# Sums of the activations on VectorE from reloaded x, weight-sum transfers at 0.7 of their pace and a reordered product in a hybrid DeltaNet, GLA and forgetting-attention layer

## The chip, the cores and the metric

The kernel runs on one core of a Trainium2 chip (trn2). The metric is the device time of one execution in microseconds (us); smaller is better. The names of the engines in the profile are PE (TensorE, matmuls), PEld (its weight loads), DVE (VectorE), ACT (ScalarE), POOL (GpSimd) and SP (SyncE, which here only issues transfers). The core has 16 DMA engines. A queue name with a q (ACTq, POOLq, SPq) is an engine's instruction queue issuing a transfer.

## The reference

One layer normalises 16 meta tokens and 512 tokens of width 2048, projects them with one wide matrix, sends the columns to three mixers in parallel, gates and joins their outputs, projects again, adds the input and normalises.

```python
h = concatenate([meta, x])                      # 528 x 2048
h0 = rms_norm(h, norm_w)
proj = h0 @ w_in                                # all heads' q, k, v, z, gates
o_dn  = gated_delta_rule_chunked(...)           # 6 heads x 128, short conv + silu on q, k, v
o_gla = gla_chunked(...)                        # 5 heads, dk 64, dv 128
o_fox = forgetting_attention(q, k, v, log_f)    # 5 heads x 128, softmax with forget bias
o = concatenate([o_dn, o_gla, o_fox])           # each times silu of its own z
out = rms_norm(h + o @ w_out, final_norm_w)[16:]
```

Everything is float32.

## The kernel before, in words

**Operands.** x is kept transposed, as 16 tiles of 128 features x 528 tokens, each times norm_w and split exactly into two float32r parts `xh[k]` and `xl[k]`. A weight block is loaded in two halves of 128 x 1024 (`load_half`), each split into `whi` (ScalarE, line 162) and `wlo` (VectorE, line 163). A product is then three matmuls: hi by hi, hi by lo, lo by hi. Plain projections run through `inproj` (matmuls of line 220).

**Pairs of blocks.** From the second forgetting-attention head on, two blocks of w_in are multiplied at once by a Strassen-like scheme with seven products in place of eight (`inproj_pair`, matmuls of line 533, 24 a product and half the tokens, HT = 264). Four of the seven use sums of weight quarters, three of them sums of quarters of x. In x the quarters are feature tiles k and k + 8, first and second half of the tokens.

- The *sums of weights* are made by transfers alone, in memory: `steps_of` issues, from GpSimd's queue, plain copies (line 448) and accumulating transfers (line 446) into `ti` for w_in, and into `tw` for the output weights, which are used in the same way at the end of the kernel. Each of these transfers is 512 KB. They are spread by a price: every `load_half` adds `rate` to an account, a copy costs 1 and an accumulating transfer 1.6, and transfers are placed while the account is positive. `AHEAD` starts them with a rate of 2 at the first DeltaNet group.
- The *sums of x* (`x_sums(ks)`, tiles `t_k`, three sums t1, t2 and t4 for each of eight k) are made by GpSimd out of xh and xl with eight additions each (tile `xd`, line 490), then split by ScalarE (line 485) and VectorE (line 486). `XSUM` says where: two k's in each of the second and third GLA pair, four in the first forgetting head.
- A fourth sum replaces the second token half of `xh[k]`, `xl[k]` for k < 8 once the plain projections no longer need it (`x_last`): `x_last(False)` forms it on VectorE in head 0 (lines 513 to 515, tiles `xe`, `xf`), `x_last(True)` splits it into place in head 1 (lines 517, 518). The product that reads it, with `ti[n, 2]`, is the fifth of the seven; the one with `ti[n, 3]` is the sixth.

**Order.** The program is written engine by engine through one scheduler that orders the instructions of every engine when the kernel is built; at run time each engine takes its own in that order. Transfers issued by GpSimd, ScalarE and SyncE stand in these engines' queues among their other instructions. Buffers come from pools: tag "row" has 7 tiles of 128 x 531, tag "six" 14 larger ones; a tile that is asked for waits until one is free.

**Stages.** First the DeltaNet gates and keys, values and queries of the first three heads, the inverse of their triangular matrices (`dn_inverse`), and the mix; then the same for the last three. The inverse runs on VectorE on small tiles and passes twice through memory: `scr`, then `sc` to `iv` (lines 694, 697), after which line 702 transposes and TensorE's `pm` (line 708) follows. Then come GLA in three pairs (`gla_pair`: scores `pss`, states `pgn`, outputs `pgo`, `pgt`), beside projections that fill TensorE, then the five forgetting heads (`fox_head`). In a forgetting head each of four query blocks passes from `pfa`, `pfd` (scores, lines 1137, 1138) through VectorE (1141, 1143), ScalarE (1146) and VectorE (1147 to 1151) to `pfx` (transposes, 1154); then `pfo` (1170 to 1173) takes all blocks. The last stage is the output projection (line 1285).

Of the kernel before, what the change touches and what calls it, by code (L numbers as in the profile page):

```python
# [8 lines left out]
F32 = mybir.dt.float32  # L9
# [4 lines left out]
AF = mybir.ActivationFunctionType  # L14
ALU = mybir.AluOpType
# [3 lines left out]
P = 128  # L19
# [4 lines left out]
T = NM + S  # L24
HT = T // 2
# [10 lines left out]
H1 = 1  # L36
# [46 lines left out]
def tile_hybrid_trunk(ctx, tc, xT, xtok, mtok, w_gate, w_in, w_out, w_dn, consts, lmask, fin_w, out, dbg=None):  # L83
    nc = tc.nc
# [12 lines left out]
    def row(name, dt=F32):  # L97
        return wk.tile([P, 3 + T], dt, tag="row", bufs=7, name=name)
# [113 lines left out]
    xh, xl = [], []  # L212
# [259 lines left out]
    def x_sums(ks):  # L472

        three = {}
        for k in ks:
            three[k] = six.tile([P, 3, T], F32R, tag="six", name=f"t_{k}")
            V.memset(three[k][:, 0, 0:1].bitcast(F32), 0.0)
        for k in ks:
            o3 = three[k]
            t = row(f"xd{k}")  # L480
            a, b = t[:, :HT], t[:, HT:T]
            B = lambda part_, i, j: (xh, xl)[part_][k + 8 * i][:, HT * j : HT * j + HT].bitcast(F32)

            def parts(n, r, hi, lo, k=k):
                A.activation(hi, r, AF.Copy, scale=-1.0)
                V.scalar_tensor_tensor(out=lo, in0=r, scalar=-1.0, in1=hi.bitcast(F32), op0=ALU.mult,
                                       op1=ALU.subtract)
                xt_[n, k] = hi, lo

            two = lambda o, p_, q_, op=ALU.subtract: G.tensor_tensor(out=o, in0=p_, in1=q_, op=op)  # L490
            two(a, B(0, 0, 1), B(0, 0, 0))
            two(b, B(1, 0, 1), B(1, 0, 0))
            two(a, a, b, ALU.add)
            parts("t1", a, o3[:, 0, :HT], o3[:, 0, HT:])
            two(b, B(0, 1, 1), a)
            two(b, b, B(1, 1, 1), ALU.add)
            parts("t2", b, o3[:, 1, :HT], o3[:, 1, HT:])
            two(a, B(0, 1, 0), b)
            two(a, a, B(1, 1, 0), ALU.add)
            parts("t4", a, o3[:, 2, :HT], o3[:, 2, HT:])  # L500

    xr = {}

    def x_last(last):

        f = lambda u: u[:, HT:].bitcast(F32)
        if not last:
            t6 = six.tile([P, 6, HT], F32, tag="six", name="xe")
            t2 = row("xf")
        for k in range(NK):  # L510
            if not last:
                xr[k] = a = t6[:, k] if k < 6 else t2[:, HT * (k - 6) : HT * (k - 5)]
                V.tensor_tensor(out=a, in0=f(xh[k + 8]), in1=f(xh[k]), op=ALU.subtract)
                V.tensor_tensor(out=a, in0=a, in1=f(xl[k + 8]), op=ALU.add)
                V.tensor_tensor(out=a, in0=a, in1=f(xl[k]), op=ALU.subtract)
            else:
                A.copy(xh[k][:, HT:], xr[k])
                V.tensor_tensor(out=xl[k][:, HT:], in0=xr[k], in1=f(xh[k]), op=ALU.subtract)  # L518

    def inproj_pair(n, c1, c2, tmp):  # L520

        h, one, two = PAIRS[n]
        b1, b2 = BLOCK_OF[one, h], BLOCK_OF[two, h]
        ta, tb = tmp[:, :HT], tmp[:, HT:]
        bank = lambda i: psb.tile([P, 512], F32, tag="b", name=f"pp{b1}_{i}")
        lo_, hi_, dead = slice(0, HT), slice(HT, T), slice(NM, HT)

        def product(p_, src, xx, first=False, cols=slice(0, HT)):

            hi, lo = load_half(src, f"{b1}_{len(order)}")  # L530
            todo = [(hi, j, i) for j in range(NK) for i in range(2)] + [(lo, j, 0) for j in range(NK)]
            for i, (wt, j, part_) in enumerate(todo):
                m = PE.matmul(p_[:, cols], wt[:, j * P : (j + 1) * P], xx[j][part_][:, cols],  # L533
                              start=first and i == 0, stop=i == len(todo) - 1, skip_group_check=True)
                order.append(m.ins)

        xs_ = lambda ks, sl: [(xh[k][:, sl], xl[k][:, sl]) for k in ks]
        sums = lambda nm: [xt_[nm, k] for k in range(NK)]
        up, dn = range(NK), range(8, 8 + NK)
        a, b = bank("a"), bank("b")  # L540
        product(a, w_in[b1, 0], xs_(up, lo_), True)
        A.copy(ta, a[:, :HT])
        product(b, w_in[b1, 1], xs_(dn, lo_), True)
        V.tensor_tensor(out=c1[:, lo_], in0=b[:, :HT], in1=ta, op=ALU.add)  # L544
        product(a, ti[n, 1], sums("t2"))
        A.copy(tb, a[:, :HT])
        d = bank("d")
        product(d, ti[n, 0], sums("t1"), True)
        V.tensor_tensor(out=tb, in0=d[:, :HT], in1=tb, op=ALU.add)
        product(a, ti[n, 2], xs_(up, hi_))  # L550
        A.copy(ta, a[:, :HT])  # L551
        c = bank("c")
        product(c, ti[n, 3], xs_(dn, hi_), True)
        V.scalar_tensor_tensor(out=c2[:, hi_], in0=d[:, :HT], scalar=-1.0, in1=ta, op0=ALU.mult, op1=ALU.subtract)
        V.tensor_tensor(out=c1[:, hi_], in0=c[:, :HT], in1=tb, op=ALU.add)
        product(a, w_in[b2, 1], sums("t4"), cols=dead)
        A.activation(c2[:, dead], a[:, dead], AF.Copy, scale=-1.0)

# [496 lines left out]
    def fox_head(h):  # L1055
# [24 lines left out]
        if h < H1:  # L1080
            evac(inproj(("fk", h)), kT)
            v = row(f"vf{h}")[:, :T]
            evac(inproj(("fv", h)), v)
            x_sums(XSUM.get(3, ()))
            vhi, vlo, v3, vm = values(v)
            evac(inproj(("fq", h), meta=False), qT, scale=float(P) ** -0.5)
        else:
            n = 2 * (h - H1) - SKIP
            if n < 0:
                evac(inproj(("fk", h)), kT)  # L1090
                evac(inproj(("fq", h), meta=False), qT, scale=float(P) ** -0.5)
            else:
                inproj_pair(n, kT, qT, qk[:, 1])
                G.tensor_tensor(out=kT, in0=kT, in1=rstd, op=ALU.mult)
                V.scalar_tensor_tensor(out=qT[:, NM:], in0=qT[:, NM:], scalar=float(P) ** -0.5, in1=rstd[:, NM:],
                                       op0=ALU.mult, op1=ALU.mult)
            v = row(f"vf{h}")[:, :T]
            zr = row(f"zfz{h}")[:, :T]
            if h == H1:
                x_last(True)  # L1100
            inproj_pair(n + 1, v, zr, qk[:, 1])
            if h == FOX_HEADS - 1:
                for i in range(6):
# [18 lines left out]
        G.affine_select(out=cm, in_=cb[:, NM:].rearrange("p (b t) -> p b t", b=NB), pattern=[[0, NB], [-1, P]],  # L1122
                        base=0, channel_multiplier=1, compare_op=ALU.is_ge, fill=BIG)

        if h == H1 - 1:
            x_last(False)
        mt = t15(f"fmt{h}", (P, NB, 2, NM), F32R)
        pm = row(f"ptm{h}", dt=F32R)[:, :S]
        G.tensor_copy(pm, zero_c.to_broadcast([P, S]))
# [46 lines left out]
            nc.sync.dma_start(out=zd[DN_HEADS + GLA_HEADS + h], in_=z)  # L1176


    AHEAD = {(0, -1): (2, (-1, -2, -3, -4, -5, -6, -7), (0, 1, 2, 3))}
    XSUM = {1: (0, 1), 2: (2, 3), 3: (4, 5, 6, 7)}  # L1180
    PM = (308, 319)

    def ahead(g, i):
# [324 lines left out]
```

## Time and profile before

| | before |
|---|---|
| three runs | 1068.16, 1080.19, 1082.35 us |
| median | 1080.19 us |
| the profiled execution, its own time | 1075.85 us |
| its span, first to last instruction | 1074.1 us |
| mean granted TensorE clock in it | 0.971 |
| GpSimd's queue of transfers (q0), bytes | 46.14 MB |

Shares of busy time are averages over stages with different limits; what a stage is limited by is read from the waits in it. The rows of the profile give a group of instructions by line, engine and operation, with the tiles written and read; the timelines give start and duration in us, and in brackets the time that the engine had been idle before and what ended that. A window's row gives the busy time of each engine in a stretch of time.

### The profile page before, as it was taken

How to read it: one execution, taken by the hardware profiler on the slowest of the kernel's cores; microseconds unless marked ns; L12 is line 12 of the kernel's file. 1: busy time of each engine (PE TensorE's matmuls, PEld its weight loads, DVE VectorE, ACT ScalarE, POOL GpSimd, SP SyncE). 2: the span in 40 equal slices, each digit the busy share in tenths (PEclk: the TensorE clock that was granted, in tenths of full speed). 3: DMA queues.
4: the chain of work that ended last, by engine and by line, in shares of the span. 5: the costliest groups of instructions: out<-in, count | busy, mean ns of one | idle time of the engine just before them, and what ended most of it. 6: DMA issues, size and time to landing. Idle time of an engine off the chain costs nothing. (4 is left out here: it accounts for less than half of the span.)

```text
span 1074.1 us, 19737 instructions
## 1 busy us (share of the span) xinstructions
PE 999.6 (93%) x7782; PEld 910.9 (85%) x7782; DVE 663.4 (62%) x1404; ACT 472.1 (44%) x1029; POOL 281.5 (26%) x304
## 2 busy tenths in 40 slices
PE   9999999989899994999999996968999998899997
PEld 7899998979899884799989985757999996688885
DVE  6365866854556882334374667875756674677673
ACT  6654532333356231333344444544454552444353
POOL 1032523521334353001334332512121201200051
PEclk9999999989999998899999999988999999999999
DMA  9665798886486699422222211333545555647534
GB/s 356 247 217 210 245 236 192 198 201 155 112 222 249 193 244 216 113 74 69 85 89 86 97 63 59 99 109 99 167 161 175 196 187 184 218 157 232 179 118 157
DMA packets 66304, 179.02 MB, mean 167 GB/s; under 512 B 13309, under 2 KB 16557, under 8 KB 65508
## 3 DMA queue, kind: packets, MB, share of 16 engines
q1 hardware_dynamic: 41776, 121.59, 33.2%
q0 software_dynamic: 13376, 46.14, 18.7%
q10 hardware_dynamic: 11060, 10.03, 3.2%
q8 instruction: 61, 1.00, 0.4%
q14 instruction: 31, 0.25, 0.1%
HBM read 167.32 MB, written 56.43 MB: 208 GB/s over the span
## 5 line engine op out<-in xcount | busy, mean ns | idle before, releaser
L220 PE MATMUL pp<-xh,wlo 128*128 128x264 f32 (+2 forms) x1120 | 272.3, 307 | 13.9 <-DVE wlo L163 13.8
L220 PE MATMUL pp<-xh,whi 128*128 128x264 f32 (+2 forms) x1120 | 276.7, 309 | 2.2 <-DVE vf L338 2.1
L220 PE MATMUL pp<-xl,whi 128*128 128x264 f32 (+2 forms) x1120 | 273.6, 308 | 0.0
L163 DVE TENSOR_TENSOR wlo<-raw,whi 128x1024 fp32r<-128x1024 f32 x131 | 168.8, 1290 | 80.1 <-ACT whi L162 75.6
L162 ACT CAST whi<-raw 128x1024 fp32r<-128x1024 f32 x131 | 137.2, 1047 | 176.9 <-PE pp L220 76.7
L220 PEld LDWEIGHTS pp<-xh,wlo 128*128 128x128 f32 x1120 | 183.9, 191 | 23.9 <-DVE wlo L163 15.7
L220 PEld LDWEIGHTS pp<-xh,whi 128*128 128x128 f32 x1120 | 184.8, 191 | 11.8 <-DVE vf L338 2.3
L220 PEld LDWEIGHTS pp<-xl,whi 128*128 128x128 f32 x1120 | 184.4, 191 | 9.1 <-issue 0.2
L347 POOL TENSOR_SCALAR stc<-cv 128x528 f32<-128x528 f32 (+1 forms) x18 | 31.2, 1735 | 129.3 <-DVE cv L569 104.2
L1309 POOL TENSOR_TENSOR accs<-accs,fw 128x512 f32<-128x512 f32 x12 | 17.6, 1510 | 113.3 <-ACT sqf L1306 113.3
L569 DVE SCALAR_TENSOR_TENSOR cv<-pb,cpk,cv 128x528 f32<-128x528 f32 (+1 forms) x54 | 41.1, 761 | 0.8
L811 POOL TENSOR_TENSOR eg<-eg,qT 128x384 f32<-128x384 f32 x8 | 9.9, 1240 | 112.8 <-DVE egl L810 112.8
L1285 PE MATMUL pa<-whio,oh 128*128 128x512 f32 x72 | 28.8, 424 | 3.5 <-DVE accs L1299 3.5
L533 PE MATMUL pp_a<-xh,whi 128*128 128x264 f32 x112 | 31.2, 307 | 0.8 <-DVE vf L544 0.8
L533 PE MATMUL pp_a<-xl,whi 128*128 128x264 f32 x112 | 31.0, 307 | 0.9 <-DVE xl L518 0.9
L533 PE MATMUL pp_a<-t,whi 128*128 128x264 f32 (+1 forms) x224 | 30.2, 284 | 0.4 <-ACT fqk L551 0.4
L1285 PE MATMUL pa<-wloo,oh 128*128 128x512 f32 x72 | 29.4, 409 | 0.0
L533 PEld LDWEIGHTS pp_a<-t,whi 128*128 128x128 f32 x224 | 28.3, 191 | 1.0 <-ACT fqk L551 0.7
L1285 PE MATMUL pa<-whio,ol 128*128 128x512 f32 x72 | 29.1, 404 | 0.0
L347 POOL TENSOR_SCALAR stdz<-zdz 128x512 f32<-128x512 f32 x6 | 11.2, 1875 | 60.9 <-DVE zdz L365 60.8
L162 ACT CAST whis<-raws 128x1024 fp32r<-128x1024 f32 x16 | 16.5, 1050 | 21.3 <-PE pq L1285 8.6
L690 DVE TENSOR_TENSOR ab<-ab 51x30 f32<-51x30 f32 (+14 forms) x60 | 21.2, 354 | 7.4 <-DMA ab<-scmeta 5.9
(482 smaller groups left out, 2161.9 us busy)
## 6 DMA issues: line engine op xcount, KB each, us to landing
raw<-in_w_in SPq DMA_DIRECT2D x103, 512.0 KB, 3.5
ti<-in_w_in POOLq DMA_DIRECT2D x42, 512.0 KB, 6.4
raw<-ti SPq DMA_DIRECT2D x28, 512.0 KB, 3.3
tw<-in_w_dn POOLq DMA_DIRECT2D x24, 512.0 KB, 6.0
ti<-ti POOLq DMA_DIRECT2D x14, 512.0 KB, 8.4
rawo<-in_w_out SPq DMA_DIRECT2D x13, 512.0 KB, 3.3
raws<-tw SPq DMA_DIRECT2D x12, 512.0 KB, 4.0
xt<-in_xtok SPq DMA_DIRECT2D x8, 512.0 KB, 9.9
```

The costliest lines, as they stand in the source:

```text
L162: pace[0] = A.copy(hi, raw).ins
L163: pace[1] = V.tensor_tensor(out=lo, in0=raw, in1=hi.bitcast(F32), op=ALU.subtract).ins
L220: mm = PE.matmul(p_[:, :nt], wt[:, j * m : (j + 1) * m], xx[k][:, t0 : t0 + nt], start=(k == 0 and wt is hi and xx is xh), stop=(k == KT - ...
L347: G.tensor_scalar_max(t, src, LOW)
L533: m = PE.matmul(p_[:, cols], wt[:, j * P : (j + 1) * P], xx[j][part_][:, cols], start=first and i == 0, stop=i == len(todo) - 1, skip_grou ...
L569: V.scalar_tensor_tensor(out=c, in0=pb[:, t0 + w : w + T], scalar=cwc[:, blk, w : w + 1], in1=c, op0=ALU.mult, op1=ALU.add)
L690: V.tensor_tensor(out=t3, in0=a3[:, j + 1 :, j : j + 1].to_broadcast([NN * 4 + H, m, j]), in1=a3[:, j : j + 1, 0:j].to_broadcast([NN * 4 + ...
L811: G.tensor_tensor(out=eg, in0=eg, in1=qT[:, :, ts], op=ALU.mult)
L1285: PE.matmul(p_, o_[:, s], w_, start=(first and n == 0), stop=(last and n == 2), skip_group_check=True)
L1309: G.tensor_tensor(out=acc[tb, cc], in0=acc[tb, cc], in1=fw[cc], op=ALU.mult)
```

## The change

Three things change together.

1. `x_sums` makes no use of GpSimd's arithmetic and of xh, xl any more. For each k, two whole rows of x (k and k + 8) are loaded again from memory, from GpSimd's queue, into row tiles `xa`, `xb`; ScalarE scales a quarter by norm_w, VectorE scales and subtracts in one operation for each of the three sums, and the split is as before. The k's 4 to 7 are divided: 4 and 5 stay in head 0, 6 and 7 move behind head 1's fk. `x_last` becomes one step in head 1 that loads its own two half rows for each k (`xe`, a row tile, again from GpSimd's queue), so that the tile `xe` of tag "six" and the 24 VectorE operations in head 0 fall away.
2. The rate of the weight-sum transfers is 1.4 in place of 2.
3. In `inproj_pair` the product with `ti[n, 3]` comes fifth and the one with `ti[n, 2]`, which reads the replaced block, sixth.

```diff
@@ x_sums
-            t = row(f"xd{k}")
-            a, b = t[:, :HT], t[:, HT:T]
-            B = lambda part_, i, j: (xh, xl)[part_][k + 8 * i][:, HT * j : HT * j + HT].bitcast(F32)
...
-            two = lambda o, p_, q_, op=ALU.subtract: G.tensor_tensor(out=o, in0=p_, in1=q_, op=op)
-            two(a, B(0, 0, 1), B(0, 0, 0))
-            two(b, B(1, 0, 1), B(1, 0, 0))
-            two(a, a, b, ALU.add)
-            parts("t1", a, o3[:, 0, :HT], o3[:, 0, HT:])
...
+            r1, r2 = row(f"xa{k}")[:, :T], row(f"xb{k}")[:, :T]
+            nc.gpsimd.dma_start(out=r1, in_=xT[:, k])
+            nc.gpsimd.dma_start(out=r2, in_=xT[:, k + 8])
+            x11, x12, x21, x22 = r1[:, :HT], r1[:, HT:], r2[:, :HT], r2[:, HT:]
+            w1, w2 = nwc[:, k : k + 1], nwc[:, k + 8 : k + 9]
+            A.activation(x11, x11, AF.Copy, scale=w1)
+            for i, (n, x, w, less) in enumerate((("t1", x12, w1, x11), ("t2", x22, w2, x12), ("t4", x21, w2, x22))):
+                hi, lo = xt_[n, k] = o3[:, i, :HT], o3[:, i, HT:]
+                V.scalar_tensor_tensor(out=x, in0=x, scalar=w, in1=less, op0=ALU.mult, op1=ALU.subtract)
+                A.activation(hi, x, AF.Copy, scale=-1.0)
+                V.scalar_tensor_tensor(out=lo, in0=x, scalar=-1.0, in1=hi.bitcast(F32), op0=ALU.mult,
                                        op1=ALU.subtract)
@@ x_last
-    def x_last(last):
-        f = lambda u: u[:, HT:].bitcast(F32)
-        if not last:
-            t6 = six.tile([P, 6, HT], F32, tag="six", name="xe")
-            t2 = row("xf")
+    def x_last():
         for k in range(NK):
-            if not last:
-                xr[k] = a = t6[:, k] if k < 6 else t2[:, HT * (k - 6) : HT * (k - 5)]
-                V.tensor_tensor(out=a, in0=f(xh[k + 8]), in1=f(xh[k]), op=ALU.subtract)
-                V.tensor_tensor(out=a, in0=a, in1=f(xl[k + 8]), op=ALU.add)
-                V.tensor_tensor(out=a, in0=a, in1=f(xl[k]), op=ALU.subtract)
-            else:
-                A.copy(xh[k][:, HT:], xr[k])
-                V.tensor_tensor(out=xl[k][:, HT:], in0=xr[k], in1=f(xh[k]), op=ALU.subtract)
+            r = row(f"xe{k}")[:, :T]
+            for i in range(2):
+                nc.gpsimd.dma_start(out=r[:, HT * i : HT * (i + 1)], in_=xT[:, k + 8 * i, HT:])
+            x12, x22 = r[:, :HT], r[:, HT:]
+            A.activation(x12, x12, AF.Copy, scale=nwc[:, k : k + 1])
+            V.scalar_tensor_tensor(out=x22, in0=x22, scalar=nwc[:, k + 8 : k + 9], in1=x12, op0=ALU.mult,
+                                   op1=ALU.subtract)
+            A.copy(xh[k][:, HT:], x22)
+            V.tensor_tensor(out=xl[k][:, HT:], in0=x22, in1=xh[k][:, HT:].bitcast(F32), op=ALU.subtract)
@@ inproj_pair
+        c = bank("c")
+        product(c, ti[n, 3], xs_(dn, hi_), True)
+        V.tensor_tensor(out=c1[:, hi_], in0=c[:, :HT], in1=tb, op=ALU.add)
         product(a, ti[n, 2], xs_(up, hi_))
         A.copy(ta, a[:, :HT])
-        c = bank("c")
-        product(c, ti[n, 3], xs_(dn, hi_), True)
         V.scalar_tensor_tensor(out=c2[:, hi_], in0=d[:, :HT], scalar=-1.0, in1=ta, op0=ALU.mult, op1=ALU.subtract)
-        V.tensor_tensor(out=c1[:, hi_], in0=c[:, :HT], in1=tb, op=ALU.add)
@@ fox_head
                 evac(inproj(("fk", h)), kT)
+                x_sums(XSUM.get(4, ()))
...
-                x_last(True)
+                x_last()
...
-        if h == H1 - 1:
-            x_last(False)
@@
-    AHEAD = {(0, -1): (2, (-1, -2, -3, -4, -5, -6, -7), (0, 1, 2, 3))}
-    XSUM = {1: (0, 1), 2: (2, 3), 3: (4, 5, 6, 7)}
+    AHEAD = {(0, -1): (1.4, (-1, -2, -3, -4, -5, -6, -7), (0, 1, 2, 3))}
+    XSUM = {1: (0, 1), 2: (2, 3), 3: (4, 5), 4: (6, 7)}
```

More of the change, by code (lines that the diff above doesn't have):

```diff
@@ L479, in x_sums @@
             o3 = three[k]
-            t = row(f"xd{k}")
-            a, b = t[:, :HT], t[:, HT:T]
-            B = lambda part_, i, j: (xh, xl)[part_][k + 8 * i][:, HT * j : HT * j + HT].bitcast(F32)
-            def parts(n, r, hi, lo, k=k):
-                A.activation(hi, r, AF.Copy, scale=-1.0)
-                V.scalar_tensor_tensor(out=lo, in0=r, scalar=-1.0, in1=hi.bitcast(F32), op0=ALU.mult,
-                                       op1=ALU.subtract)
-                xt_[n, k] = hi, lo
@@ L490, in x_sums @@
-            two = lambda o, p_, q_, op=ALU.subtract: G.tensor_tensor(out=o, in0=p_, in1=q_, op=op)
-            two(a, B(0, 0, 1), B(0, 0, 0))
-            two(b, B(1, 0, 1), B(1, 0, 0))
-            two(a, a, b, ALU.add)
-            parts("t1", a, o3[:, 0, :HT], o3[:, 0, HT:])
[L495 to L500, printed above, removed]
@@ L502, in tile_hybrid_trunk @@
-    xr = {}
-    def x_last(last):
-        f = lambda u: u[:, HT:].bitcast(F32)
-        if not last:
-            t6 = six.tile([P, 6, HT], F32, tag="six", name="xe")
-            t2 = row("xf")
-        for k in range(NK):
-            if not last:
-                xr[k] = a = t6[:, k] if k < 6 else t2[:, HT * (k - 6) : HT * (k - 5)]
-                V.tensor_tensor(out=a, in0=f(xh[k + 8]), in1=f(xh[k]), op=ALU.subtract)
-                V.tensor_tensor(out=a, in0=a, in1=f(xl[k + 8]), op=ALU.add)
-                V.tensor_tensor(out=a, in0=a, in1=f(xl[k]), op=ALU.subtract)
-            else:
-                A.copy(xh[k][:, HT:], xr[k])
-                V.tensor_tensor(out=xl[k][:, HT:], in0=xr[k], in1=f(xh[k]), op=ALU.subtract)
+            r1, r2 = row(f"xa{k}")[:, :T], row(f"xb{k}")[:, :T]
```

## The prediction

> **What bounds the kernel now.** I read the page first, then TensorE's waits, then the stages in which those waits stand.
>
> ```profile
> span 1074.1 us, 19737 instructions
> PE 999.6 (93%) x7782; PEld 910.9 (85%) x7782; DVE 663.4 (62%) x1404; ACT 472.1 (44%) x1029; POOL 281.5 (26%) x304
> ```
>
> TensorE is the bound: 999.6 of 1074.1 us. The change takes no matmul away, so it can only act on the 74.5 us in which TensorE idles, and on its clock behind such gaps. The list of who waited for whom, TensorE's largest rows:
>
> ```profile
> PE pm L708 <- DVE iv L702: 16.4, 1, 16.4
> PE pp L220 <- DVE wlo L163: 13.8, 4, 5.6
> PE pfx L1154 <- DVE fp L1151: 8.5, 1, 8.5
> PE pfx L1154 <- DVE fmt L1149: 6.7, 2, 3.6
> ```
>
> These four rows are 45.4 us. The first is the inverse of the second DeltaNet group. The windows (us; busy time and count of PE, PEld, DVE, ACT, POOL; granted clock, DMA share, GB/s) show that stage and, last, the first group's:
>
> ```profile
> 410.00:415.00 5.00, 5.00 (x44) 5.00 (x43) 0.00 (x0) 0.00 (x0) 5.00 (x7) 1.00 1.07 302
> 420.00:425.00 5.00, 0.00 (x0) 0.00 (x0) 0.00 (x0) 1.89 (x3) 0.87 (x1) 0.54 1.18 203
> 430.00:435.00 5.00, 2.75 (x54) 2.69 (x55) 1.87 (x5) 2.65 (x5) 1.28 (x2) 0.50 0.27 71
> 435.00:440.00 5.00, 5.00 (x24) 4.52 (x24) 3.24 (x5) 2.31 (x4) 0.00 (x0) 0.75 0.93 204
> 215.00:220.00 5.00, 5.00 (x43) 5.00 (x42) 4.68 (x12) 0.00 (x0) 0.00 (x0) 1.00 0.65 190
> ```
>
> While the second inverse waits, the 16 DMA engines are full (share 1.07 to 1.18; for the first group 0.65). Behind the gap the clock is 0.50, then 0.75: 2.75 us and 5.00 us of busy time lose 1.4 and 1.25 us, so this gap costs 16.4 + 2.6 = 19 us.
>
> **Part one, the pace 2 to 1.4.** Each half weight block pays 1.4 instead of 2, so the transfers of the weight sums come 1/0.7 = 1.43 times as far apart and last longer. The timelines of ACT's queue, VectorE and GpSimd at the two inverses:
>
> ```profile
> 216.06 0.26 ACTq L694 DMA_DIRECT2D sc<-ab  x1
> 222.29 0.40 ACTq L697 DMA_DIRECT2D iv<-sc  x1
> 225.01 0.58 DVE L702 STREAM_TRANSPOSE iv<-iv 128x384 f32<-128x384 f32 x1 [4.28 <-DMA iv<-sc]
> 229.12 0.27 DVE L701 STREAM_TRANSPOSE um<-xm 32x96 f32<-32x96 f32 x1 [3.54 <-DMA xm<-sc]
> 406.98 0.26 ACTq L694 DMA_DIRECT2D sc<-ab  x1
> 417.92 0.39 ACTq L697 DMA_DIRECT2D iv<-sc  x1
> 431.62 0.58 DVE L702 STREAM_TRANSPOSE iv<-iv 128x384 f32<-128x384 f32 x1 [21.98 <-DMA iv<-sc]
> 413.40 2.75 POOL L446 DMA_DIRECT2D tw<-tw  x3
> ```
>
> The round trip through memory (write sc, read iv) takes 225.0 - 216.1 = 8.9 us in the first group and 431.6 - 407.0 = 24.6 us in the second, where accumulating transfers of tw stand beside it. In the changed program's instruction order, GpSimd issues one accumulating transfer (of ti) where it issued three between the last two gate products ahead of the write, and then seven plain tw copies in a row, at the spot of the 413.40 row. So the write should take the first group's time; the read meets seven copies. Bounds: 24.6 us again (nothing saved), or 8.9 us (15.7 saved, the wait falls to 0.7, and the 2.6 us of clock go too). Between them I take 15 us: the wait falls by 9.6 and the clock loss by 2.4, together **-12** (bounds 0 and -18). Late next is the transpose um, which in the first group held VectorE another 3.54 us and TensorE like this:
>
> ```profile
> PE pp L220 <- DVE wlo L163: 5.4, 1, 5.4
> ```
>
> The first group's own transfers thin out as well, but its trip was not crowded: **-2** (bounds 0 and -6). The sums must still be in time. ti ended at 296.5 us (line L446's last issue), tw at 432.9:
>
> ```profile
> L446 POOL DMA_DIRECT2D ti<-ti x14: 916/1253/2676, 208.9 to 296.5; - x14
> L446 POOL DMA_DIRECT2D tw<-tw x8: 869/1093/1590, 401.1 to 432.9; - x8
> L448 POOL DMA_DIRECT2D ti<-in_w_in x28: 486/488/769, 2.5 to 142.5; - x28
> DMA to landing us min/median/max: 3.8/5.6/9.9
> ```
>
> Stretched by 1.43 that is about 425 and 620 us; the first pair product, which needs ti, stands behind the 672.63 row below, and the output products, which need tw, later still. What moves into the stage of 500 to 700 us I cost at nothing: its DMA share is 0.26 (row below), so weight loads and these transfers pass beside each other; if that cover is gone, each late load is a wait for wlo of the sizes above, up to 5.6 us.
>
> **Part two, the sums of x.** GpSimd loses its 56 operations of xd:
>
> ```profile
> 500.00:700.00 200.00, 11.23 (x24) 9.18 (x24) 52.21 (x56) 0.97 0.26 84
> L486 DVE SCALAR_TENSOR_TENSOR t<-xd,t x24: 416/425/830, 551.2 to 690.3; 128x264 fp32r<-128x264 f32 x24
> L513 DVE TENSOR_TENSOR xe<-xh,xh x6: 423/424/426, 712.9 to 714.6; 128x264 f32<-128x264 f32 x6
> 718.60 0.41 ACT L517 CAST xh<-xe 128x264 fp32r<-128x264 f32 x1 [5.64 <-DVE xe L515]
> ```
>
> (The first row is the window of xd's instructions alone: DVE, ACT, POOL; a few records are missing, the code has 64.) VectorE gains 3 operations for each of 8 k's, 24 x 0.425 = 10.2 us, and loses 24 - 8 = 16 of x_last, 16 x 0.424 = 6.8 us: net +3.4. ScalarE gains 8 + 8 of 0.41 us, +6.6. VectorE is busy 62%, so these lie beside TensorE's work unless a chain waits. GpSimd gains 32 issues; none like them is in the trace, so by the L448 and L446 rows 0.5 to 1.25 us each, 16 to 40 us in all; I take 0.7 (128 rows lie nearer the cheap ones), 22 us. The first 12 stand ahead of GpSimd's products in the gated linear attention, which wait for ScalarE anyway; cost 0, and if not, up to one late issue each. What GpSimd's additions cost others shows here (VectorE, GpSimd, TensorE timelines):
>
> ```profile
> 664.46 4.09 DVE L990 TENSOR_TENSOR gdm<-gdm,gqk 64x16 f32<-64x16 f32 x1
> 665.68 1.44 POOL L490 TENSOR_TENSOR xd<-xh,xd 128x264 f32<-128x264 f32 x2
> 671.36 1.21 DVE L163 TENSOR_TENSOR wlo<-raw,whi 128x1024 fp32r<-128x1024 f32 x1
> 672.63 0.79 PE L220 MATMUL pp<-xh,wlo 128*128 128x512 f32 x1 [5.64 <-DVE wlo L163]
> 660.00:680.00 20.00, 13.88 (x148) 11.22 (x148) 19.96 (x33) 10.16 (x23) 12.32 (x12) 0.83 0.08 28
> ```
>
> A 64x16 operation stood 4.09 us on VectorE while GpSimd added; wlo behind it came late, TensorE lost 5.64 us and, at clock 0.83, 13.88 x 0.17 = 2.4 us more. That 8 us goes. In the changed order the last products before head 0's attention (pgo, pgt) have no pair product between them any more and wait for their short chains; I give back 2: **-6** (bounds -9 and +1).
>
> **Part three, head 0's attention and the replaced block.** The sums of k = 6, 7 are now made after head 1's fk, from row tiles that head 0's attention must free first (7 in all). So in the changed order the product t1 stops after 12 of 24 matmuls, and the whole attention of head 0 (pfa to pfo) stands on TensorE without a pair matmul in it; before, 65 of them stood there. The stage before:
>
> ```profile
> 707.87 0.29 PE L1137 MATMUL pfa<-fqk 128*128 128x16 f32 x2
> 708.01 0.47 PE L1138 MATMUL pfd<-fqk 128*128 128x128 f32 x2
> 727.21 0.43 DVE L1141 CUSTOM_DVE_ANT_0 fp<-pfa,fc 128x272 f32<-128x272 f32 x1
> 731.63 0.56 DVE L1141 CUSTOM_DVE_ANT_0 fp<-pfa,fc 128x400 f32<-128x400 f32 x1
> 700.00:720.00 20.00, 10.21 (x77) 9.50 (x75) 16.14 (x43) 9.44 (x23) 3.12 (x2) 0.85 0.36 114
> 720.00:740.00 20.00, 14.81 (x79) 13.64 (x80) 10.98 (x44) 6.94 (x17) 1.95 (x2) 0.72 0.14 41
> 756.95 2.92 PE pp_c L533 x24
> ```
>
> One query block follows the other by 731.63 - 727.21 = 4.4 us: four are 17.7, and 5 more until pfo is done and the loads of k = 7 (behind xb's issue) have become sums: 23 us, of which TensorE fills some 5 with its own short products (0.8 a block by the first two rows, and pfo): 18 idle. Then x_last. Its 16 loads stand behind all this in GpSimd's queue (the issue of k = 7's second half waits there for a mask that needs a load of its own, and behind the 16 stands the product of vf with rstd, for which TensorE's transposes pvf wait). A k then passes load, ScalarE, VectorE, ScalarE, VectorE: 4 x 0.42 = 1.7 us after landing, and the last three k's start late. The exchange of the fifth and sixth product puts 2.92 us of cover in front; the rest of t1 and t2 is 2 more. I take a wait of 6 (bounds 0 and 52, the latter below). In the later pairs the exchange only moves one copy and one sum past each other under the next 2.92 us product: 0. Idle 24, clock as now about 5: 29 lost, on 19 us of work (112 pair matmuls at 2.92/24 and the 5). What goes: idle 9.8 + 5.2 = 15.0 us in the two windows, and clock 10.21 x 0.15 + 14.81 x 0.28 = 5.7, together 20.7 (the 24 x_last operations stood in this chain). Net **+8** (bounds -3, with no tail and no wait of x_last, and +54).
>
> Sum: -12 - 2 - 6 + 8 = -12 against the profiled execution's own 1075.85 us (its span 1074.1 and 1.75 around it): **1064 us**. That execution lies inside the runs shown, 1068.16 to 1082.35, 4 us under their median 1080.19; I leave the forecast at 1064, 1.5% under the median. Two per cent, about what a measurement of this kernel can tell from no change, are 1058.6 and 1101.8.
>
> **Rivals.** *All crowding goes* (the trip falls to 8.9 us, -18; first group -6; contention -9; and x_last waits 0, net +2): -31, **1045**. For it: the share 0.65 beside the short trip. Against: seven copies in a row, and a stage that lost cover.
>
> *x_last in single file* (slower). Place: the 16 loads on GpSimd ahead of the sixth product; five row tiles are free at first, the last three k's need tiles of the first ones. If each k had to pass alone, 5.6 to landing (the median above) + 1.7 = 7.3, eight take 58 us; under a cover of 6, 52 are left, 46 over my 6: **1110**. It decides from (38 + 12)/8 = 6.3 us a k. For it: each load waits in an in-order queue. Against: five tiles overlap.
>
> *The pace saves nothing* (the change doesn't do what it says): the burst of copies holds the read as the accumulations did. +14: **1078**. For it: copies move as many bytes as an accumulation reads from its source. Against: the write and half the burst are gone. The Trainium skill (DMA: Bandwidth & Descriptors, section "Queues, rings and completion order") speaks for this one: each DMA engine goes round the queues that have work, a packet at a time, so a read of small pieces on ACT's queue would be slowed by any busy neighbour; the trips of 8.9 and 24.6 us at shares 0.65 and 1.18 do not settle it.
>
> *Half clock through head 0*: gaps of 2 to 4 us in a row keep the clock at 0.50 (as at 430 us) for all 19 us of work between pfa of head 0 and of head 1: +19 instead of +5: **1078**. The Trainium skill (TensorE: Matmul & The Clock Gate, section "What's actually happening") would have it so, halving the clock after an idle window of about 3.4 us; the windows here show 0.72 to 0.85 in this stage.
>
> **How the numbers follow.** Forecast 0.40 (1052 to 1078; 0.14 of it under 1058.6), all crowding goes 0.28, single file 0.18, pace saves nothing 0.07, half clock 0.07. Faster by over 2%: 0.14 + 0.28 = 0.42; within: 0.26 + 0.14 = 0.40; slower: 0.18. The range 1040 to 1100 leaves out the lower edge of the second case and most of the third.
>
> **What would show it.** Right: pm's wait under 8 us; no wait of 5 us for wlo near 672; one stretch of about 23 us with TensorE mostly idle at head 0, then a wait of the sixth product for xl of about 6. Wrong: pm still over 14; more than 30 us for xl; new waits for wlo between 450 and 640, where the tw transfers now stand.

## The result, and the profile after

The changed kernel takes **1045.67 us** (median of 4 executions, 1042.38 to 1046.40) against 1079.41 us before (1068.16 to 1082.35): ratio 0.970, 95% interval 0.9628 to 0.9773. It is 3% faster. Medians here are over all executions; a ratio leaves out executions more than 1.5% above the fastest of their kernel, so it can differ a little from the quotient of the medians.

From the page of the changed kernel, its span and its busy times:

```profile
span 1043.6 us, 19779 instructions
PE 998.6 (96%) x7782; PEld 908.4 (87%) x7782; DVE 659.1 (63%) x1412; ACT 479.2 (46%) x1045; POOL 239.5 (23%) x280
```

TensorE's busy time is the same to 1.0 us; its idle time went from 74.5 to 45.0 us. That is 29.5 of the 30.5 us by which the span fell. The list of TensorE's waits after the change, and the windows (columns as in the prediction) of the second inverse:

```profile
PE pfx L1139 <- DVE fmt L1134: 11.5, 4, 3.8
PE pgt L1029 <- ACT gqk L1026: 3.8, 3, 2.4
PE pp_a L519 <- ACT xh L503: 3.7, 4, 2.2
PE pp L220 <- DVE wlo L163: 2.9, 1, 2.9
395.00:400.00 5.00, 5.00 (x33) 4.53 (x32) 3.53 (x9) 1.05 (x1) 1.56 (x2) 1.00 0.57 182
400.00:405.00 5.00, 5.00 (x44) 5.00 (x43) 0.12 (x1) 0.69 (x2) 5.00 (x6) 1.00 0.70 175
405.00:410.00 5.00, 5.00 (x83) 4.82 (x82) 2.83 (x6) 4.88 (x9) 3.12 (x7) 1.00 0.99 354
```

The 16.4 us wait of pm for iv is gone from the list altogether, the wait for wlo fell from 13.8 to 2.9 us, and TensorE is full at clock 1.00 while the second inverse passes through memory. The timelines of ACT's queue, VectorE and GpSimd show why:

```profile
396.59 0.26 ACTq L680 DMA_DIRECT2D sc<-ab  x1
402.32 0.39 ACTq L683 DMA_DIRECT2D iv<-sc  x1
404.20 3.08 POOL L448 DMA_DIRECT2D tw<-in_w_dn  x6
405.53 0.58 DVE L688 STREAM_TRANSPOSE iv<-iv 128x384 f32<-128x384 f32 x1 [5.40 <-DMA iv<-sc]
```

The round trip takes 405.5 - 396.6 = 8.9 us, what the first group's took before the change. The six copies of tw are issued 1.9 us behind the read. While the read is under way (402.32 to 405.50 us) only 2 of their packets pass, as the DMA view of that stretch shows (packets, MB, share of the 16 engines; q10 carries the read, q0 the copies):

```profile
q10 hardware_dynamic: 1664, 0.21, 42.8%
q0 software_dynamic: 2, 0.07, 6.7%
```

Head 0's attention, though, is stripped as forecast (TensorE's timeline, then windows):

```profile
666.03 0.45 PE L1122 MATMUL pfa<-fqk 128*128 128x16 f32 x2
671.51 0.45 PE L1139 MATMUL pfx<-ident,fp 128*128 128x128 f32 x1 [3.79 <-DVE fmt L1134]
685.24 1.09 PE L1139 MATMUL pfx<-ident,fp 128*128 128x128 f32 x4 [2.92 <-DVE fmt L1134]
689.89 0.41 PE L1155 MATMUL pfo<-fphi,vlo 128*128 128x256 f32 x1
703.01 0.59 PE L519 MATMUL pp_a<-xh,whi 128*128 128x264 f32 x1 [2.25 <-ACT xh L503]
660.00:680.00 20.00, 8.56 (x40) 7.11 (x39) 8.46 (x38) 8.07 (x28) 3.19 (x4) 0.59 0.19 53
680.00:700.00 20.00, 14.98 (x78) 12.43 (x76) 14.13 (x35) 11.03 (x27) 9.99 (x19) 0.73 0.48 144
700.00:720.00 20.00, 16.07 (x98) 14.57 (x99) 11.57 (x21) 9.64 (x19) 4.65 (x5) 0.74 0.43 151
```

From 666 to 690 us the attention's own short products run alone. The rest of t1 and t2 and the fifth product follow, and the sixth product waits for the replaced block (the row at 703.01).

To place the 30.5 us, TensorE's timeline of every kernel below was cut at the same instructions: the first pm of each group (the two inverses), the last pss (the end of the gated linear attention's products), the first output product pa, and the last matmul. Each number is the difference of two start times, in us:

| kernel | to 1st inverse | to 2nd inverse | to last pss | to first output product | to the end |
|---|---|---|---|---|---|
| before | 235.1 | 197.1 | 256.3 | 194.0 | 183.4 |
| after | 228.0 | 179.2 | 247.5 | 201.1 | 179.6 |
| e1_pace_only | 229.2 | 187.4 | 261.9 | 195.0 | 181.9 |
| e2_old_pace | 230.5 | 198.6 | 248.9 | 201.9 | 178.8 |
| e3_pause | 234.5 | 188.8 | 255.4 | 193.9 | 183.8 |
| e4_cover | 229.2 | 180.0 | 255.1 | 202.2 | 179.9 |
| e5_held | 228.3 | 176.6 | 248.6 | 200.7 | 181.5 |
| e6_early | 228.8 | 185.3 | 252.0 | 202.8 | 181.6 |
| e7_held_at_2 | 235.4 | 179.3 | 258.2 | 194.7 | 183.8 |
| e8_sums_on_v | 228.9 | 179.4 | 261.5 | 189.7 | 181.5 |
| e9_sums_only | 229.4 | 177.1 | 249.6 | 196.4 | 180.5 |
| e10_old_last | 228.0 | 177.1 | 248.8 | 203.2 | 179.5 |
| e11_no_exchange | 228.8 | 176.6 | 249.5 | 193.8 | 179.3 |
| e12_both_held | 226.0 | 182.6 | 253.4 | 193.0 | 181.7 |

After against before: -7.1, -17.9, -8.8, +7.1, -3.8. One trace stands for each kernel, so differences of 2 us between rows are not read.

These columns are times, and the two kernels do not do the same work in each of them. After the change 51 matmuls of pair products start ahead of the last pss (6 before) and 24 behind the first output product (none before), so head 0's stage holds 69 fewer; at 2.92/24 us each, 45 of them are 5.5 us and 24 are 2.9 us. What the stages lose is therefore read from TensorE's idle time in them and from its busy time at clock 0.50, half of which is lost (the last column here runs to the end of the span):

| idle + lost to the clock, us | to 1st inverse | to 2nd inverse | to last pss | to first output product | to the end |
|---|---|---|---|---|---|
| before | 11.2 + 2.0 | 19.8 + 0.5 | 13.7 + 6.2 | 15.3 + 5.5 | 14.6 + 3.4 |
| after | 6.9 + 0.7 | 0.3 + 2.7 | 3.7 + 2.7 | 23.2 + 10.6 | 10.8 + 0.0 |
| change of the sum | -5.6 | -17.3 | -13.5 | +13.0 | -7.2 |

The stage up to the last pss gained more than its time shows, and head 0's stage lost more.

### The profile page after: what moved, and what is told of

Read it like the earlier page. It is cut to its first block, busy times and chain, and to the rows that moved or that the text cites. A ratio compares the mean times of both kernels' runs of the same rounds, so it can differ in the third digit from the quotient of the medians.

```text
span 1043.6 us, 19779 instructions
## 1 busy us (share of the span) xinstructions
PE 998.6 (96%) x7782; PEld 908.4 (87%) x7782; DVE 659.1 (63%) x1412; ACT 479.2 (46%) x1045; POOL 239.5 (23%) x280
## 4 chain that ended last, share of the span: by engine, by line
PE 73%; DMA 5%; DVE 5%; ACT 4%; issue 2%; POOL 1%; ACTq 0%; SPq 0%; DVEq 0%; POOLq 0%
PE pp L220 37%; PE pp_a L519 7%; PE pq L1270 4%; PE pt L1270 4%; PE pa L1270 3%; PE ps L1270 2%; PE pp_b L519 2%; PE pp_d L519 2%; PE pp_c L519 1%; DMA accs<-in_xtok 1%; DMA eg<-gd 1%; PE pr L1270 1%; ACT whi L162 1%; PE pss L945 1%; DMA raw<-in_w_in 1%
## 5 line engine op out<-in xcount | busy, mean ns | idle before, releaser
L220 PEld LDWEIGHTS pp<-xh,whi 128*128 128x128 f32 x1120 | 183.8, 190 | 10.9 <-DVE fqk L338 1.8
L519 PE MATMUL pp_a<-xl,whi 128*128 128x264 f32 x112 | 29.5, 297 | 1.1 <-DVE xl L504 1.1
L519 PEld LDWEIGHTS pp_a<-xh,whi 128*128 128x128 f32 x112 | 21.8, 195 | 8.3 <-ACT xh L503 4.7
L1270 PE MATMUL pa<-whio,oh 128*128 128x512 f32 x72 | 26.7, 403 | 2.0 <-ACT whio L162 2.0
L347 POOL TENSOR_SCALAR stdz<-zdz 128x512 f32<-128x512 f32 x6 | 10.1, 1687 | 63.8 <-DVE zdz L365 63.3
```

The costliest lines, as they stand in the source:

```text
L220: mm = PE.matmul(p_[:, :nt], wt[:, j * m : (j + 1) * m], xx[k][:, t0 : t0 + nt], start=(k == 0 and wt is hi and xx is xh), stop=(k == KT - ...
L347: G.tensor_scalar_max(t, src, LOW)
L1270: PE.matmul(p_, o_[:, s], w_, start=(first and n == 0), stop=(last and n == 2), skip_group_check=True)
```

## The experiments

**One part at a time.** e1: the kernel before with

```diff
-    AHEAD = {(0, -1): (2, ...
+    AHEAD = {(0, -1): (1.4, ...
```

> The kernel before with one edit: the pace of the weight-sum transfers 1.4 instead of 2. Theory A (the pace carries most of the gain; in the two traces the second DeltaNet inverse starts 25.5 us earlier after the change, and only the pace acts ahead of it): the round trip sc to iv in the second group takes about 9 us, the wait of pm for iv is under 1 us, and the time falls by about 25 us, to some 1054; the wait for wlo near the first pair products and the gaps at head 0 stay as before. Theory B (the sums on GpSimd are what held the kernel, through VectorE): under 8 us are gained here.

Measured: 1048.53 us (four executions: 1047.09, 1047.84, 1049.22 and 1065.42), ratio 0.9736 (0.9682 to 0.979). The pace alone carries most of the gain: theory A by the time, 31 us against the 25 expected. The trip of the three short executions was not traced. The wait for wlo near the first pair products (5.7 us) stays, as expected. The profiled execution is the longest of the four, and in it the trip takes 20.5 us and pm waits 10.5. Its timelines, the view of iv, its waits, and the DMA view from 403.69 to 415.94 us:

```profile
395.49 0.26 ACTq L694 DMA_DIRECT2D sc<-ab  x1
403.02 2.98 POOL L448 DMA_DIRECT2D tw<-in_w_dn  x6
403.69 0.39 ACTq L697 DMA_DIRECT2D iv<-sc  x1
DMA to landing us min/median/max: 12.3/12.3/12.3
PE pm L708 <- DVE iv L702: 10.5, 1, 10.5
q0 software_dynamic: 192, 3.15, 69.0%
q10 hardware_dynamic: 1664, 0.21, 10.9%
```

Here the write took 8.2 us, the six copies were issued 0.7 us ahead of the read, and the read took 12.3 us to land instead of 3.2, while 192 packets of the copies passed instead of 2. That gave the theory for e5 and e6: a race.

e2: the changed kernel with the pace 2 again.

> The changed kernel with one edit: the pace back at 2. Theory A: the wait of pm for iv is back at about 16 us, and the time lies only some 5 us under before (contention and output stage -12, head 0 +7), about 1074. Theory B: at least 15 us of the gain stay, 1064 or less.

Measured: 1076.07 us (ten executions, 1064.29 to 1083.33), ratio 0.9939 (0.9889 to 0.9989). The wait of pm is back at 16.6 us. At that pace parts two and three together are worth 0.6%; theory A holds, theory B falls.

e3: the kernel before at pace 2, paused over the second group's queries and inverse.

```diff
+    ..., (1, 1): (0,), (1, 3): (2,)}
```

> The kernel before at pace 2, with the pace set to 0 from behind the second group's values to behind its inverse, so that no accumulating transfer is issued between the write of sc and the landing of iv; 2 again after it. If the neighbours of the round trip alone make the wait (theory A1), the wait of pm for iv falls under 1 us and about 19 us are gained (1061), while the 6 us that the first 400 us gained after the change stay out. If the density of the transfers over the whole stage counts (theory A2: DMA engines behind by tens of microseconds), the trip stays above 15 us and under 8 us are gained.

Measured: 1076.17 us (ten executions, 1057.73 to 1083.71), ratio 0.9868 (0.9822 to 0.9913). It decides nothing: the pause put the schedule of transfers back instead of clearing the trip. GpSimd issued five transfers of the accumulating kind at 413.36 us, beside the read at 413.6, which took 9.0 us; pm waited 6.9.

**The race.** e5: the changed kernel with the six copies held behind the trip.

```diff
+            if hold and kind in (None,):
+                tc.add_manual_dep(d.ins, hold[0].name, ...
...
+        if g == 1:
+            hold.append(G.tensor_copy(t15("hold", (32, 32)), um[:, 0]).ins)
```

The kind None marks the plain copies of tw; the small copy of um can run only when the trip is over.

> The changed kernel with one edit: the six copies of tw that GpSimd issues about 2 us behind the read of iv (404.2 against 402.3 us in its trace) are held behind a 32x32 copy of um on GpSimd, which waits for the round trip to be over. Theory R (a race: whoever reaches the DMA queues first, the copies or the read of iv, decides; in the execution profiled with the pace alone the copies went at 403.0 and the read at 403.7, and the read took 12.3 us instead of 3.2): the read takes 3 to 4 us, pm waits under 1 us, and no execution lies above 1050; the median stays at 1043 to 1047. Rival (the transfers issued earlier are what slows the read): the read still takes over 8 us in some executions, and the spread stays up to 1065.

e6: the changed kernel with those copies sooner, by moving the two fills of kq ahead of them from GpSimd to VectorE.

```diff
     for t in kq:
-        G.memset(t, 0.0)
+        V.memset(t, 0.0)
```

> The changed kernel with one edit: the two fills of kq are made by VectorE instead of GpSimd, so that the same six copies of tw are issued 2.7 us sooner, at about 401.5 us, ahead of the read of iv. Theory R: the read takes 10 to 14 us in every execution, pm waits some 8 to 12 us, and with 2.5 us of clock the time is 1055 to 1060. Rival: 2.7 us of shift change nothing, 1042 to 1047.

Measured: e5 1047.43 us (1045.14 to 1052.27), ratio 0.9763 (0.9694 to 0.9831); e6 1055.85 us (1054.36 to 1060.42), ratio 0.9842 (0.9775 to 0.991). From the timelines, the view of iv and the waits of e6:

```profile
400.32 3.00 POOL L448 DMA_DIRECT2D tw<-in_w_dn  x6
403.01 0.39 ACTq L683 DMA_DIRECT2D iv<-sc  x1
DMA to landing us min/median/max: 10.4/10.4/10.4
PE pm L694 <- DVE iv L688: 8.0, 1, 8.0
```

The median of e6 is 10 us above the changed kernel's, and its shortest execution 8 us above the changed kernel's longest. Counted from the write, the six copies come 2.6 us sooner (5.0 instead of 7.6 us behind it); the write then takes 7.7 us instead of 5.7, so the read is issued 2.7 us behind the copies and takes 10.4 us. In e5 the read takes 3.0 us and pm does not wait; its median is 0.4 us and one execution, at 1052, 2 us above what was expected, so not all of the spread is this race. The changed kernel's traced execution won the race and its other three are as short, so holding the copies had nothing to bring over it.

e7: the kernel before at pace 2, with only the transfers tw<-tw held in the same way.

> The kernel before, pace still 2, with one edit: the accumulating transfers tw<-tw that GpSimd issued from 401 us on are held behind a 32x32 copy of um on GpSimd, so that none is issued between the write of sc and the landing of iv. No other transfer moves. Theory A1 (the neighbours of the round trip make the wait, not the pace): the trip takes about 9 to 12 us, pm waits under 3 us, and some 16 us are gained, 1060 to 1064. Theory A2 (the pace over the whole stage): the trip stays above 18 us, 1074 or more.

Measured: 1062.59 us (ten executions, 1049.95 to 1069.29), ratio 0.9828 (0.9773 to 0.9884). Its timelines:

```profile
404.61 0.26 ACTq L700 DMA_DIRECT2D sc<-ab  x1
411.03 0.39 ACTq L703 DMA_DIRECT2D iv<-sc  x1
414.04 0.58 DVE L710 STREAM_TRANSPOSE iv<-iv 128x384 f32<-128x384 f32 x1 [6.76 <-DMA iv<-sc]
415.72 0.92 POOL L448 DMA_DIRECT2D tw<-tw  x1
```

A trip of 9.4 us at the old pace, no wait of pm, and 15 us less in the median: theory A1. The neighbours of the trip make the wait, and half of what the pace brought can be had without it. Of the other part some 6 us show in the first column: 235.4 us here, 228 to 229 at 1.4. That this is the pace is not certain, since e2 has 230.5 at pace 2. The rest is not placed, as no short execution of e1 was traced.

**The sums.** e8: pace 1.4, copies held, no reload, and

```diff
-            two = lambda o, p_, q_, op=ALU.subtract: G.tensor_tensor(...)
+            two = lambda o, p_, q_, op=ALU.subtract: V.tensor_tensor(...)
```

> The kernel before with pace 1.4, the copies of tw held behind the round trip as in the run of the changed kernel of this call, and the 64 additions of xd made by VectorE instead of GpSimd; x is not reloaded and x_last stays as it was. If what the new sums gain is the end of the contention between GpSimd and VectorE, the 64x16 operation gdm falls from 4 to 6 us to about 0.2, the wait of some 5.6 us for wlo behind it goes, and, with the attention of head 0 covered as before, the time is at most that of the changed kernel: 1035 to 1044. If the 27 us that VectorE takes over (64 x 0.42) cost more than the reloads do, it is 1048 or more.

Measured: 1049.25 us (1046.41 to 1052.10), ratio 0.9769 (0.969 to 0.9847), the second branch by its time. The stage up to the last pss takes 261.5 us, as long as in e1, but holds more: 89 matmuls of pair products start in it, 6 in e1, and 83 of them are 10 us of work. Behind the last py TensorE idles 10.8 us in it, against 16.2 in e1, 13.7 before and 3.7 after the change. So additions on VectorE brought a part of what the reload brings; fewer waits and more cover are not told apart here. The views of the tiles gdm and gt before, after the change, and in e8 (min/median/max, ns):

```profile
L990 DVE TENSOR_TENSOR gdm<-gdm,gqk x3: 753/1280/4089, 553.2 to 664.5; 128x16 f32<-128x16 f32 x2, 64x16 f32<-64x16 f32 x1
L980 POOL TENSOR_TENSOR gt<-gt,gqk x3: 2477/3054/5070, 553.9 to 663.2; 128x512 f32<-128x512 f32 x2, 64x512 f32<-64x512 f32 x1
```

```profile
L976 DVE TENSOR_TENSOR gdm<-gdm,gqk x3: 157/162/163, 530.6 to 636.7; 128x16 f32<-128x16 f32 x2, 64x16 f32<-64x16 f32 x1
L966 POOL TENSOR_TENSOR gt<-gt,gqk x3: 1852/1852/1972, 526.3 to 633.4; 128x512 f32<-128x512 f32 x2, 64x512 f32<-64x512 f32 x1
```

```profile
L998 DVE TENSOR_TENSOR gdm<-gdm,gqk x3: 1277/1291/1293, 533.6 to 647.0; 128x16 f32<-128x16 f32 x2, 64x16 f32<-64x16 f32 x1
L988 POOL TENSOR_TENSOR gt<-gt,gqk x3: 3629/4309/4997, 530.6 to 643.2; 128x512 f32<-128x512 f32 x2, 64x512 f32<-64x512 f32 x1
```

With the additions on VectorE the small operation no longer stands 4 us, but GpSimd's gt takes 3.6 to 5.0 us, and 1.9 only with the reload. The crowding is between the two engines whichever of them adds. That the reload ends it because the 64 additions are gone is argued, not shown: VectorE still subtracts 24 times, and no run leaves out those alone. The Trainium skill (SBUF — State Buffer, section "Who interferes with whom") says that a VectorE instruction with two SBUF inputs contends with a GpSimd instruction that reads SBUF, and that issue order decides who waits. These rows agree with the first, on both sides (gdm 4.09 us before, gt 5.0 us in e8); they do not show the order of issue.

**Head 0.** e4: the changed kernel with the sums of k = 6, 7 ahead of head 0's attention again.

```diff
-    XSUM = {1: (0, 1), 2: (2, 3), 3: (4, 5), 4: (6, 7)}
+    XSUM = {1: (0, 1), 2: (2, 3), 3: (4, 5, 6, 7)}
```

> The changed kernel with one edit: the sums of k = 6 and 7 made ahead of head 0's attention again, as before, instead of behind head 1's fk. By the prediction's part three the 25 us of mostly idle TensorE at head 0 come from that place: with it undone, 24 matmuls of the third product lie beside the first gaps and the loads of x_last run under the attention: 5 to 10 us gained over the changed kernel, about 1038. Rival: the replaced block (x_last) is what keeps cover away, since the sixth product and all behind it wait for it: within 3 us of the changed kernel.

Measured: 1054.18 us (1049.10 to 1060.62), ratio 0.9791 (0.9718 to 0.9864): slower than the changed kernel, where a gain was expected. In the profiled execution the copies were issued at 403.70 and the read at 403.74. The read's first packets still came ahead of the copies' (before 405.2 us 339 packets of the read pass and none of the copies); iv landed in 4.8 us and pm waited 2.4, but the small read xm behind it held um until 414.8 (after the change 406.0), and with it wlo, for which TensorE waited 4.2 us. Of the 11 us by which this execution is longer, 7.6 stand in the third column. The stage of head 0 takes 202.2 us: the rival, as the cover does not come back; the time, 8 us longer by the medians, is not within the rival's 3 us, and the trace puts that on the trip.

Then three kernels with the copies held: e9 (old x_last, reloaded sums, those of 6 and 7 ahead of head 0, exchange kept), e10 (the changed kernel with old x_last) and e11 (e9 without the exchange).

> The kernel before with the pace 1.4, the copies of tw held behind the round trip, the sums of x made by VectorE from reloaded x with those of k = 6 and 7 ahead of head 0's attention, and the exchanged product; x_last stays as it was before (three VectorE operations a k at head 0, no reload). Theory X (the reloaded x_last, which needs row tiles that head 0's attention holds, is what strips that attention of pair matmuls; with the sums of 6 and 7 alone put back the stage from the last pss to the first output product still took 202 us against 194 before): that stage falls to about 194 us, the earlier stages stay as after the change, and the time is 1036 to 1041. Rival (the loss at head 0 is the price of the reloaded sums): the stage stays at 200 or more, 1045.

> The changed kernel with the copies of tw held and x_last as it was before; the sums of 6 and 7 stay behind head 1's fk. If each of the two (late sums, late x_last) alone takes the cover away, the stage from the last pss to the first output product stays at 198 to 201 us and the time at 1043 to 1047; if x_last alone does, it is 194 us and 1037 to 1040.

> The first kernel of this call with the product of the replaced block fifth again. The prediction priced the exchange at nothing once x_last isn't late: within 2 us of that kernel. If the exchange is worth the 2.92 us of cover by itself at each of the later pairs, it is 3 us or more slower.

Measured: e9 1043.47 us (1042.06 to 1048.87), ratio 0.9713 (0.9617 to 0.9809); e10 1046.67 (1043.72 to 1048.94), 0.9727 (0.965 to 0.9804); e11 1041.63 (1037.95 to 1048.23), 0.9688 (0.9603 to 0.9774). Stage of head 0: 196.4, 203.2 and 193.8 us against 200.7 in e5. Late sums alone (e10) and late x_last alone (e4) each take the cover away; it returns only with both put back, in e9 in part. In idle time and clock together the stage loses 33.1 us in e5, 33.4 in e4, 37.3 in e10, 29.2 in e9 and 24.4 in e11, against 20.8 before. The time of e9 was expected at 1041 at most: the 4 us regained are less than the 7 forecast, and neither branch fits. The exchange is worth nothing that these runs can tell (1.8 us between the medians, within their spread).

e12: e11 with the transfers of ti held behind the first group's trip as well.

> The last kernel of the call before (product order as before, old x_last, sums of x on VectorE from reloaded x, pace 1.4, copies of tw held behind the second round trip), and now the transfers of ti held behind the first group's round trip too, where one of them was issued 0.2 us ahead of the read of iv, which took 6.2 us. Theory R: that read takes about 3 us as well, wlo behind the transposes on VectorE is no longer late (2.97 us of TensorE and about 2 us of clock), the second inverse stays without a wait, and the time is 1035 to 1040. Rival: the nine transfers then issued in a row behind the trip delay weight loads or the gates by as much, 1041 or more.

Measured: 1044.85 us (six executions, 1043.04 to 1046.67), ratio 0.9725 (0.9683 to 0.9766): the rival. From its waits up to 420 us (in two windows) and ScalarE's timeline:

```profile
PE pp L220 <- DVE wlo L163: 0.8, 1, 0.8
PE py L820 <- DVE zz L816: 4.4, 1, 4.4
262.47 0.52 ACT L806 ACTIVATE eg<-eg 128x384 f32<-128x384 f32 x1 [8.15 <-DMA eg<-gd]
```

The wait for wlo fell from 3.0 to 0.8 us, and behind the nine transfers that now come in a row another load, eg, came late: zz, behind it on VectorE, cost 4.4 us. The wait had moved. The best kernel, e11, is 4 us under the changed one by the medians, but the kernel before, run beside it, was 6 us shorter as well (1073.21 us); by the ratios, 0.9688 and 0.970, the two cannot be told apart.

## Why the prediction was right, and where its terms were off

The time lies inside the range (1040 to 1100) and on the side that had the larger chance (faster, 0.42); the forecast itself, 1064, was 18 us too high. It is the time of the rival "all crowding goes" (1045), though not its make-up: that one had head 0 at +2 and nothing after it. By the table of idle time and clock, the forecast took the gains of the second inverse and of the contention 7 and 5 us too small and the loss at head 0 5 us too small, and 10 us more (two waits for zz, the output stage) were not in its sum. That the contention and head 0 cancel is luck.

- **Second inverse, -12 (bounds 0 and -18): -19.** The wait of 16.4 us and 2.6 us of half clock behind it (in the third column) went entirely. In the second column two waits for zz, 3.2 us, went as well, which the sum did not have. The step that failed is the point between the bounds: "the read meets seven copies" took the place of the copies in GpSimd's queue for their time. They stand behind three fills (1.4 + 2.7 us) and come 1.9 us after the read. In these traces the second group's read took 2.9 to 4.8 us or 9.0 to 13.9, the longer ones all with transfers issued ahead of it; 15 us for the trip stood for neither. The rival "the pace saves nothing" names a real mechanism: e6 shows it, 10 us dearer, with copies in place of accumulations. The Trainium skill (DMA: Bandwidth & Descriptors, section "Queues, rings and completion order") says that DMA engines go round the queues with work, a packet at a time. The traces fit it: 3.2 us for the read where 2 packets of the copies pass beside it, 12.3 where 192 do.
- **First group, -2 (bounds 0 and -6): -3.4.** The first column lost 7.1 us, 5.6 of them idle time and clock; but 2.2 us of the half clock behind its last wait now fall into the second column. The 5.4 us wait for wlo fell to 2.9 and the stages ahead of it ran without their small waits. "Its trip was not crowded" was wrong: before, three transfers of ti were issued 0.1 us behind its read of iv, which escaped them (2.7 us), while xm behind it held um until 229.1 us. After the change one transfer of ti is issued 0.1 us ahead, and the trip is longer than before, 12.2 us (211.0 to 223.2) instead of 8.9; in e12, without that transfer, it is 10.1.
- **Contention at 664 to 673, -6 (bounds -9 and +1): -10.9** from the last py to the last pss, outside its bounds:

```profile
525.70:688.80 163.10, 149.43 (x1870) 133.88 (x1868) 106.77 (x209) 70.61 (x186) 68.89 (x66) 0.97 0.25 81
498.50:655.00 156.50, 152.77 (x1915) 138.44 (x1913) 101.21 (x225) 75.58 (x191) 31.85 (x36) 0.98 0.61 162
```

These are the two windows, before and after. Idle time falls from 13.7 to 3.7 us and the loss to the clock from 3.6 to 2.7. The time falls by 6.6 us only, since 45 more matmuls of pair products run in it; that this looks like the forecast is luck. The place was right and the 5.6 us wait for wlo went, but the term counted that wait and its clock alone, and most of the shorter waits of this stage for VectorE and ScalarE went too. It is part two that does it: e2 idles 3.9 us here at the old pace, e1 16.2 at the new one. The reason was half right, since additions on VectorE keep part of the waits (e8). The transfers of tw that moved into this stage, put at nothing, cost no wait for wlo: the DMA share rose from 0.25 to 0.61, and TensorE's waits here name no wlo. Of the small terms, ScalarE's +6.6 was +7.1, VectorE's +3.4 was -4.3, an issue by GpSimd 0.54 us instead of 0.7.
- **Head 0, +8 (bounds -3 and +54): +13.0.** The stretch of 24 us between pfa and pfo is there, and the sixth product's waits for the replaced block are 3.7 + 1.1 us where 6 was taken. The mis-sized term is the clock: idle time in 660 to 720 us is 60 - 39.6 = 20.4 us (24 forecast), the clock cost 8.56 x 0.41 + 14.98 x 0.27 + 16.07 x 0.26 = 11.7 us (5 forecast, 19 in the half-clock rival). In shorter windows the granted clock is 0.50 from 664 to 690 and from 702 to 711 us, and 1.00 between and behind them, so 0.59 to 0.74 are mixtures of the two. The rule of a halved clock behind an idle window, which the prediction took from the Trainium skill (TensorE: Matmul & The Clock Gate, section "What's actually happening"), held for part of the stage. The stage's time rose by 7.1 us only, since 69 matmuls of pair products had left it. The cause named, the late sums alone, was incomplete (e4, e10).
- **Single file** did not happen. The view of xe:

```profile
L498 POOL DMA_DIRECT2D xe<-in_xT x16: 536/536/552, 689.0 to 699.8; - x16
L504 DVE TENSOR_TENSOR xl<-xe,xh x8: 421/430/434, 693.7 to 708.4; 128x264 fp32r<-128x264 f32 x8
```

Eight k's took 708.8 - 689.0 = 19.8 us, 2.5 a k, where it would have decided from 6.3.

- **Not in the sum: the output stage, -3.8 in time, -7.2 in idle time and clock.** After the change 24 matmuls of pair products, 2.9 us, run in it beside the output products. Across the kernels this stage takes 178.8 to 183.8 us; no run was made for its cause, and it stays open.

## What to carry to other kernels

A long wait for a small transfer is priced by what is issued in the few microseconds ahead of it, on any queue: read the issue times, not the mean DMA share, and price both orders. Differences of start times mix waits with work that has moved; idle time and granted clock in the same stretch tell them apart. Holding a burst of transfers behind the one that the critical chain needs costs one small instruction (e7 gained 15 us by it), but the burst then meets whatever is loaded next (e12). Work that replaces data in place needs its buffers to be free, and takes the cover from the stage that holds them.

## What the runs showed of the hardware

The read of iv (192 KB on ACT's queue, 1664 packets with the small read xm) took 3.2 us when six copies of 512 KB were issued 1.9 us behind it, 4.8 when they went at the same time (403.70 and 403.74), 12.3 when they were 0.7 us ahead and 10.4 when 2.7 us ahead. In the quick ones of 3.0 and 3.2 us GpSimd's queue had 0 and 6.7% of the DMA engines' time during the read, in the slow ones of 10.4 and 12.3 us 69%. Moving the issue of the copies by under 3 us against the write moved the kernel by 10 us (e6). The four executions of e1, three at 1047 to 1049 us and the traced one, which lost the race, at 1065, would fit a race that falls differently from execution to execution; the three were not traced, so this is not shown.
